# Output-norm sums two blocks later and spread over a block, three output gates held back, decay rows in float32r, memory scaling on GpSimd, in a decoder-layer kernel

## The chip, the core and the metric

The kernel runs on one core of a Trainium2 chip. A core has five engines that run side by side and wait for each other through semaphores: TensorE (PE in the profile; PEld is its weight load), VectorE (DVE), ScalarE (ACT), GpSimd (POOL) and SyncE (SP), which here only issues transfers. The metric is the device time of one execution in microseconds. Before the change it is 1560.88 us, the median of three runs between 1558.69 and 1561.04.

## The reference

The kernel computes one layer of a hybrid decoder for 256 prompt tokens and 8 sampled tokens (264 columns), with a model width of 2048, all in float32:

```python
xn = rmsnorm(x, g_mix);  z = xn @ w_in          # rgx 1024, rgg 1024, q 512, k 512, v 1024, o 1024, gates 8
h_rg = rglru(causal_conv(z_rgx), ...)           # RG-LRU group
y_rg = rmsnorm(h_rg * gelu(z_rgg), g_rg_out)
q, k, v, logi, logf = ...                       # mLSTM group: 4 heads, key 128, value 256
logD = bcum[:, None] - bcum[None, :] + li ;  m_t = max(...)   # running maximum of the gates
qk = (q @ k.T) * exp(logD - m_t)                # prompt: chunkwise; sample: state C0 (8 x 4 x 128 x 256)
h_ml = rmsnorm(num / max(|den|, exp(-m_t)), g_ml_out)         # per head, over 256 values
y_ml = h_ml * sigmoid(z_o)
x = x + concat(y_rg, y_ml) @ w_out
mk, mv = rmsnorm(mem) @ w_k, rmsnorm(mem) @ w_v # 256 memory tokens
x = x + cross_attention(rmsnorm(x) @ w_q, mk, mv) @ w_o       # sample tokens use cached memory keys
x = x + swiglu(rmsnorm(x));  y = rmsnorm(x)
```

The output also has the new states of both groups and the memory keys and values.

## The kernel before

**Tiling.** Activations lie with the features on the 128 partitions and the 264 tokens along the row. Each weight matrix is streamed in column blocks of 128 columns, 1 MB each for 2048 rows. The matrices of the first projection come as rgx (blocks 0 to 7), gates (block 8, half as long), q and k (9 to 16), v (17 to 24), rgg (25 to 32) and o (33 to 40); then `w_out`, the memory projections, cross attention and the feed-forward part follow.

**Weights.** SP loads each block as two halves (`raw`, five buffers). A half is split into two float32r parts by `split_half`: ACT copies it into the high part of a tile `W` (ACTIVATE `W<-raw`), and DVE subtracts to get the low part (TENSOR_TENSOR `W<-raw,W`). There are four `W` tiles, so ACT may write the next one only when PE has read the oldest. `mm3` multiplies one 128-row chunk by three matmuls (high by high, high by low, low by high) into a PSUM bank. A full block has 16 chunks, so 48 of these weight matmuls; in what follows a place on PE is given as the count of weight matmuls before it. Block 9 begins at 416, and each block from there on to block 40 takes 48.

**Banks.** Four PSUM banks, `mm`, take the blocks in turn, and four, `ax`, take all side work. Block i writes the bank that block i-4 used, so its first matmul waits until the result of block i-4 has been read out.

**Order.** The loop over `steps` writes block after block. At the start of a block it evacuates the block before (`pend`, with high priority), then splits the halves of a later block, writes the matmuls, and lets side generators run (`pump`): `rg_gen` (RG-LRU), `ml_gates` (decays of the mLSTM), `ml_prompt` (four heads of the prompt), the sample head states, `ml_norm` (norm of the mLSTM output), `mem_gen` (memory norm). `later` and `drip` put a few small matmuls between two chunks of a block. A list scheduler then sets each engine's order; each engine runs its instructions in that order.

**Places that the change touches.** `first_norm` sums the squares of x over partitions (`token_sums`, six matmuls of one column with `ones`), and spreads the root over the tile (`spread`). `ml_prompt` spreads each head's decay row with one float32 matmul (`bc`), whose stationary operand is a broadcast column of `ident`. A head of `ml_prompt` takes an `ax` bank for the decay (`bc`), one for the scores (`sps`) and one for the numerator (`nps`). The sample states (`ml_sample`) write a small table of decays and vectors to a scratch in memory (`scr`), read it back broadcast (`B<-scr`), fetch the states (`B<-c0T`) and write them back (`o_sc<-B`), all on POOL's queue. `ml_norm` sums each head's squares (`ax<-ones,B`) at the start of block 31. `mem_gen` multiplies 16 chunks of the memory by the reciprocal root (`B<-B,lt`) on DVE and splits each (`B<-B,vecs`).

Of the kernel before, what the change touches and what calls it, by code (L numbers as in the profile page):

```python
# [17 lines left out]
P = 128  # L18
# [65 lines left out]
def layer_kernel(ctx: ExitStack, tc, xT, memT, vec, wrg, w_in, w_out, w_q, w_k, w_v, w_o,  # L84
# [131 lines left out]
    def mm3(ps, a, b, start, stop):  # L216
        ah, al = a
        bh, bl = b
        pe.matmul(ps, ah, bh, start=start, stop=False)
        pe.matmul(ps, ah, bl, start=False, stop=False)  # L220
        pe.matmul(ps, al, bh, start=False, stop=stop)

    st = {}

# [69 lines left out]
    dve.memset(ones, 1.0)  # L294
    ones_r = const.tile([P, P], F32R, name="ones_r")
    dve.tensor_copy(ones_r, ones)
    warm_act = const.tile([P, 1], F32, name="warm_act")
    act.activation(warm_act, ones[:, 0:1], AF.Square)

# [10 lines left out]
    vecs = const.tile([P, NV], F32, name="vecs")  # L310
    act.dma_start(vecs[:, 0:16], vec[:, 0:16])
    act.dma_start(raw_half(0, 0)[:, 0:512], w_in[0][:, 0:512])
    act.dma_start(vecs[:, 16:], vec[:, 16:])

    def V(name, j=0, w=1):
        o = _V[name][0] + j
# [273 lines left out]
    def ml_gates():  # L590
# [14 lines left out]
        dve.tensor_tensor_scan(M[:, :T], g[:, :T], g[:, :T], 0.0, op0=OP.max, op1=OP.max)  # L605
        dve.tensor_add(b[:, :T], b[:, :T], M[:, :T])
        dve.tensor_scalar(M[:, :T], M[:, :T], -1.0, None, op0=OP.mult)
        dve.tensor_copy(mrow[:, 0:1], b[:, T - 1: T])

        s = slice(T, N)  # L610
# [52 lines left out]
    def ml_prompt():  # L663
        qk = ml["qk"]
        yield STEP
        kt = B([P, 2, H, P])
        for tb in range(2):
            ps = bank("ax")
            for h in range(H):
                pe.transpose(ps[:, h * P: h * P + P], qk(4 + h)[:, tb * P: tb * P + P], ident)  # L670
            act.activation(kt[:, tb].rearrange("p h d -> p (h d)"), ps, AF.Copy)
            yield STEP
        while "gates" not in ml or not ml["gates"].done:
            yield STEP
        R = ml["R"]
        M = R(6)[0:4, :T]
        for h in range(H):
            sel = ident[0:4, h: h + 1].to_broadcast([4, P])
            bc = bank("ax")
            pe.matmul(bc[:, :T], sel, M, start=True, stop=True)  # L680
            sps = bank("ax")
            q, k = qk(h), qk(4 + h)
            pe.matmul(sps[:, 0:256], k[:, 0:P], q[:, 0:T], start=True, stop=True)
            pe.matmul(sps[:, 256:384], k[:, P:T], q[:, P:T], start=True, stop=True)
            w = B([P, 1024])
            E, Pm, kw = w[:, 0:384], w[:, 384:768], w[:, 768:1024]
            ml["w", h] = (Pm, kw)
            yield STEP
            dve.tensor_scalar(E[:, 0:256], bc[:, 0:T], gcol[:, 0, h: h + 1], 0.0, op0=OP.add, op1=OP.min)
            dve.tensor_scalar(E[:, 256:384], bc[:, P:T], gcol[:, 1, h: h + 1], 0.0, op0=OP.add, op1=OP.min)  # L690
            act.activation(E, E, AF.Exp)
            dve.tensor_mul(E[:, 0:128], E[:, 0:128], mask)
            dve.tensor_mul(E[:, 256:384], E[:, 256:384], mask)
            dve.tensor_mul(Pm, sps[:, 0:384], E)
            act.activation(kw[:, 0:P], kt[:, 0, h, :], AF.Copy, scale=E[:, 255:256])
            act.activation(kw[:, P:T], kt[:, 1, h, :], AF.Copy, scale=E[:, 383:384])
            yield 1.0
            ml["pn"] = h + 1
# [118 lines left out]

    def ml_norm():

        while not (ml["pg"].done and ml["sg"].done):  # L820
            yield STEP
        hh = hT["t"]
        a = B([P, H, N])
# [21 lines left out]
                dve.tensor_mul(f, f, r)  # L845
            return i

        k = later(*[lambda h=h: sums(h) for h in range(H)])
        while k[1]:
            yield STEP  # L850
        for h in range(H):
# [19 lines left out]
    def proj(src, rhs, evac, cols=2048, n=N, need=()):  # L871

        def f(i):
            ps = bank()
            w = W(i)
            nch = cols // P
            for c in range(nch):
                d = st.pop("drip", None)
                if c == 0:
                    d = st.get("edge")  # L880
                if d is None:
                    mm3(ps[:, :n], w(c), rhs(c), c == 0, c == nch - 1)
                else:
                    with tc.issue_after(d.ins):
                        mm3(ps[:, :n], w(c), rhs(c), c == 0, c == nch - 1)
                drip()
            return ps
        steps.append((src, cols, f, evac, need))

# [86 lines left out]
    def mem_gen():  # L976
# [12 lines left out]
        st["mem"] = Side()  # L989
        for c in range(KC):  # L990
            x = raw(c)
            dve.tensor_mul(x, x, r)
            split(*st["mem"](c), x, V("g_mem", c))
            yield 0.7

# [306 lines left out]
            sp.dma_start(r[:, h % 2 * 512: h % 2 * 512 + 512], w_in[0][:, h * 512: h * 512 + 512])  # L1302
    for q in range(1, 4):
        load_x(4 * q, 4 * q + 4)
        if q < 3:
            load_piece(q)

# [26 lines left out]
    def first_norm():  # L1334
# [11 lines left out]
            act.activation(rstd, ps[:, :N], AF.Copy)  # L1346
            return i

        later(sums, after=4)
        k = later(scale, after=9)  # L1350
        while k[1]:
            yield STEP
        yield 0.1
# [2 lines left out]
    for i, (src, cols, pef, evf, need) in enumerate(steps):  # L1356
        load_piece(i + LD - 1)
        if i == 5:
            finish(lambda: fn.done)
            st["rg"] = side(rg_gen(), 0)  # L1360
        for q in need:
            if q in st:
                finish(lambda: st[q].done)
        if i != 4:
            with tc.high_priority(300):
                for e, x in pend:
                    e(x)
# [10 lines left out]
                    square(q)  # L1378
        if i == 3:
            fn = side(first_norm(), -1)  # L1380
        if i == 5:
            with tc.issue_after(st["split"].ins), tc.issue_after(st["low"].ins):
                rg_coef()
        if evf is not None:
# [120 lines left out]
```

## Time and profile before

| what | value |
|---|---|
| runs | 1558.69, 1560.88, 1561.04 us; median 1560.88 us |
| profiled execution | 1558.76 us |
| its span | 1557.1 us (1.66 us lie outside it) |
| granted clock | 0.995 |
| PE busy | 1537.7 us (99%) |
| DVE busy | 1055.1 us (68%) |
| ACT busy | 781.7 us (50%) |
| POOL busy | 123.1 us (8%) |
| chain that ended last | PE 96%, DVE 2%, ACT 1%, DMA 1% |

The span is the time between the first and the last recorded instruction. A timeline row gives the start of a group of like instructions, the time from the start of the first to the end of the last, the engine, the line, the operation, the tile names (written before the arrow, read after it), the shape, the count, and in brackets how long the engine had been idle and whose work ended the wait. All operations recorded by the helper have line L63.

### The profile page before, as it was taken

Reading aid. Unit: us, or ns where it says so; the run is one execution under the profiler, and the core shown is the slowest. Engines: PE = TensorE matmul, PEld = TensorE weight load, DVE = VectorE, ACT = ScalarE, POOL = GpSimd, SP = SyncE. Lnnn points to the kernel's source line nnn. Section 1 sums busy time; section 2 is a strip of 40 time slices with the busy share of each in tenths; the row PEclk is TensorE's granted clock in tenths of the full one; section 3 lists DMA queues with packets and bytes.
Section 4 is the critical chain, followed back from the end, with each engine's and each line's share of the span. In section 5 each row is a group of like instructions: output and inputs, shape, how many; then the busy total and the mean of one; then the engine's idle time right before and its main releaser. Section 6 shows DMA issues by size and latency. Waiting matters only on the chain.

```text
span 1557.1 us, 30109 instructions
## 1 busy us (share of the span) xinstructions
PE 1537.7 (99%) x12094; PEld 1502.1 (96%) x12094; DVE 1055.1 (68%) x1998; ACT 781.7 (50%) x1229; POOL 123.1 (8%) x190
## 2 busy tenths in 40 slices
PE   9999989999999999999999999999999999999997
PEld 8999989999999888899999999999999999999997
DVE  7976977787699989876665555455555555555554
ACT  6565755665455566655544444334444433444463
POOL 0001210000133343310000000000000000000000
PEclk9999989999999999999999999999999999999999
DMA  7647974547789887955555555555555555555463
GB/s 292 195 154 245 304 259 147 185 157 242 254 303 342 324 299 250 336 166 177 184 178 181 189 178 189 180 186 183 183 186 180 185 182 187 180 188 179 160 183 104
DMA packets 92171, 326.00 MB, mean 209 GB/s; under 512 B 10784, under 2 KB 11216, under 8 KB 92032
## 3 DMA queue, kind: packets, MB, share of 16 engines
q1 hardware_dynamic: 76464, 270.44, 51.5%
q0 software_dynamic: 15136, 53.16, 9.4%
q8 instruction: 94, 1.54, 0.4%
q10 hardware_dynamic: 432, 0.50, 0.1%
q14 instruction: 45, 0.37, 0.1%
HBM read 312.78 MB, written 11.28 MB: 208 GB/s over the span
## 4 chain that ended last, share of the span: by engine, by line
PE 96%; DVE 2%; ACT 1%; DMA 1%; issue 0%; DVEq 0%; ACTq 0%
PE mm L63 91%; PE ax L63 5%; DVE B L63 1%; DVE W L63 1%; ACT W L63 0%; DMA xres<-xT 0%; DMA vecs<-vec 0%; ACT B L63 0%; ACT t L63 0%; DVE c L63 0%; DVE xres L63 0%; DVE acc_x L63 0%; DVE t L63 0%; ACT rstd L63 0%; DVEq L1482 0%
## 5 line engine op out<-in xcount | busy, mean ns | idle before, releaser
L63 PE MATMUL mm<-B,W 128*128 128x264 f32 (+2 forms) x11008 | 1368.0, 286 | 1.7 <-DVE W L63 0.8
L63 PEld LDWEIGHTS mm<-B,W 128*128 128x128 f32 x11008 | 1343.7, 188 | 13.9 <-DVE W L63 1.0
L63 DVE TENSOR_TENSOR W<-raw,W 128x1024 fp32r<-128x1024 f32 (+2 forms) x518 | 622.3, 1204 | 363.5 <-ACT W L63 362.9
L63 ACT ACTIVATE W<-raw 128x1024 fp32r<-128x1024 f32 (+2 forms) x518 | 536.6, 1038 | 661.1 <-PE mm L63 461.6
L63 PE MATMUL mm<-W,B 128*128 128x512 f32 x384 | 92.7, 395 | 0.0
L63 PEld LDWEIGHTS mm<-W,B 128*128 128x128 f32 x384 | 70.9, 188 | 15.9
L63 DVE TENSOR_TENSOR t<-mm,rstd 128x264 f32<-128x264 f32 x104 | 44.9, 433 | 45.0 <-PE mm L63 44.5
L1397 POOL TENSOR_TENSOR B<-B,rstd 128x264 f32<-128x264 f32 x4 | 2.8, 744 | 855.1 <-ACT rstd L63 855.1
L63 DVE TENSOR_TENSOR xres<-xres,mm 128x264 f32<-128x264 f32 x80 | 34.3, 429 | 38.6 <-PE mm L63 38.6
L63 DVE SCALAR_TENSOR_TENSOR B<-B,dw 128x256 f32<-128x256 f32 x128 | 55.6, 490 | 4.0 <-ACT dw L63 4.0
L63 DVE SCALAR_TENSOR_TENSOR dw<-B,qsm,dw 128x256 f32<-128x256 f32 x96 | 49.8, 527 | 0.4
L63 PE MATMUL ax<-B,B 128*128 128x256 f32 (+3 forms) x288 | 48.2, 308 | 0.1
L63 PEld LDWEIGHTS ax<-B,B 128*128 128x128 f32 x288 | 40.6, 190 | 3.4 <-issue 0.6
L1046 POOL TENSOR_TENSOR dr<-dw,dr 128x256 fp32r<-128x256 f32 x32 | 34.1, 1070 | 106.9 <-ACT dr L63 105.8
L63 ACT ACTIVATE B<-xres,vecs 128x264 fp32r<-128x264 f32 (+1 forms) x64 | 31.1, 503 | 3.6 <-DMA vecs<-vec 1.5
L1035 POOL DMA_DIRECT2D B<-kcT x32 | 17.3, 541 | 146.3 <-DVE B L63 137.4
L63 ACT ACTIVATE B<-t 128x264 fp32r<-128x264 f32 (+1 forms) x60 | 24.3, 410 | 4.3 <-DVE t L63 4.2
L63 ACT ACTIVATE t<-xres 128x264 f32<-128x264 f32 x45 | 18.6, 414 | 15.4 <-DVE xres L63 15.4
L63 ACT ACTIVATE dw<-B,qsm 128x256 f32<-128x256 f32 x32 | 16.2, 507 | 17.8 <-DVE B L63 10.9
L63 ACT ACTIVATE t<-t 128x264 f32<-128x264 f32 (+1 forms) x61 | 24.9, 408 | 0.6 <-DVE t L63 0.5
L63 DVE SCALAR_TENSOR_TENSOR B<-xres,vecs,B 128x264 fp32r<-128x264 f32 x48 | 22.6, 491 | 3.7 <-ACT B L63 3.7
L63 ACT ACTIVATE t<-B,B 128x128 f32<-128x128 f32 x64 | 21.4, 389 | 4.8 <-DMA B<-scr 4.8
(153 smaller groups left out, 657.0 us busy)
## 6 DMA issues: line engine op xcount, KB each, us to landing
raw<-w_gu SPq DMA_DIRECT2D x176, 512.0 KB, 3.5
raw<-w_in SPq DMA_DIRECT2D x80, 512.0 KB, 4.3
raw<-w_d SPq DMA_DIRECT2D x80, 512.0 KB, 3.6
raw<-w_out SPq DMA_DIRECT2D x32, 512.0 KB, 3.7
B<-kcT POOLq DMA_DIRECT2D x32, 512.0 KB, 8.4
raw<-w_q SPq DMA_DIRECT2D x32, 512.0 KB, 4.2
B<-vcT POOLq DMA_DIRECT2D x32, 512.0 KB, 8.4
raw<-w_k SPq DMA_DIRECT2D x32, 512.0 KB, 6.9
```

Of the source, the lines that this page charges most:

```text
L63: return f(*a, **k)
L1035: pool_e.dma_start(kc, kcT[h, b])
L1046: pool_e.tensor_sub(wr[:, 1], acc, wr[:, 0].bitcast(F32))
L1397: e.tensor_mul(st["y"](c), st["y"](c), r)
```

## The change

There are six edits.

1. First norm: `vecs[:, 16:]` is loaded from SP's queue behind the second quarter of x; it was on ACT's queue. The token sums go in after eight drips (four before) and the spread ten drips later (nine). `finish(fn.done)` and the start of `rg_gen` are one block apart from where they were: `rg_gen` begins at block 5 and the norm's end is required at block 6, and blocks 4 and 5 both skip the evacuation.
2. A drip is issued after the matmul of its chunk (`issue_after(m.ins)`).
3. `ml_norm` starts only from block 33 on (`st["i"] < 33`), and its four sums begin after three drips.
4. Blocks 34 and 35 skip the evacuation, so the first three output gates (blocks 33 to 35) are evacuated at the start of block 36.
5. The decay rows: the row M is split into two float32r parts (`mhl`, one ACT copy and one DVE subtraction of 4x256), `ident_r` is a float32r copy of four rows of `ident`, and a decay is spread by two float32r matmuls in place of the float32 one.
6. The 16 multiplications of `mem_gen` are put on POOL (`pool_e.tensor_mul`).

```diff
@@ mm3 @@
-        pe.matmul(ps, al, bh, start=False, stop=stop)
+        return pe.matmul(ps, al, bh, start=False, stop=stop)
@@ constants @@
+    ident_r = const.tile([4, H], F32R, name="ident_r")
+    dve.tensor_copy(ident_r, ident[0:4, 0:H])
...
-    act.dma_start(vecs[:, 16:], vec[:, 16:])
@@ ml_gates @@
+        mhl = ml["mhl"] = B([P, 2, T], F32R)[0:4]
+        act.activation(mhl[:, 0], M[:, :T], AF.Copy)
+        dve.tensor_sub(mhl[:, 1], M[:, :T], mhl[:, 0].bitcast(F32))
@@ ml_prompt @@
-            sel = ident[0:4, h: h + 1].to_broadcast([4, P])
+            sel = ident_r[:, h: h + 1].to_broadcast([4, P])
             bc = bank("ax")
-            pe.matmul(bc[:, :T], sel, M, start=True, stop=True)
+            pe.matmul(bc[:, :T], sel, mhl[:, 0], start=True, stop=False)
+            pe.matmul(bc[:, :T], sel, mhl[:, 1], start=False, stop=True)
@@ ml_norm @@
-        while not (ml["pg"].done and ml["sg"].done):
+        while not (ml["pg"].done and ml["sg"].done) or st["i"] < 33:
             yield STEP
...
-        k = later(*[lambda h=h: sums(h) for h in range(H)])
+        k = later(*[lambda h=h: sums(h) for h in range(H)], after=3)
@@ proj @@
                 if d is None:
-                    mm3(ps[:, :n], w(c), rhs(c), c == 0, c == nch - 1)
+                    m = mm3(ps[:, :n], w(c), rhs(c), c == 0, c == nch - 1)
                 else:
                     with tc.issue_after(d.ins):
-                        mm3(ps[:, :n], w(c), rhs(c), c == 0, c == nch - 1)
-                drip()
+                        m = mm3(ps[:, :n], w(c), rhs(c), c == 0, c == nch - 1)
+                if drips:
+                    with tc.issue_after(m.ins):
+                        drip()
@@ mem_gen @@
-            dve.tensor_mul(x, x, r)
+            pool_e.tensor_mul(x, x, r)
@@ loads at the start @@
+        if q == 2:
+            sp.dma_start(vecs[:, 16:], vec[:, 16:])
@@ first_norm @@
-        later(sums, after=4)
-        k = later(scale, after=9)
+        later(sums, after=8)
+        k = later(scale, after=10)
@@ loop over the blocks @@
         if i == 5:
+            st["rg"] = side(rg_gen(), 0)
+        if i == 6:
             finish(lambda: fn.done)
-            st["rg"] = side(rg_gen(), 0)
...
-        if i != 4:
+        st["i"] = i
+        if i not in (4, 5, 34, 35):
             with tc.high_priority(300):
                 for e, x in pend:
                     e(x)
...
-        if i == 5:
+        if i == 6:
             with tc.issue_after(st["split"].ins), tc.issue_after(st["low"].ins):
                 rg_coef()
```

Three places show how the order moves.

PE at the sums of the output norm. Before, they stand behind the first chunk of block 31 (`mm_2873`, from weight matmul 1472):

```order
L63 MATMUL mm_2873<-B_137,W_2797 128x264
L63 MATMUL mm_2873<-B_138,W_2797 128x264
L63 MATMUL mm_2873<-B_137,W_2797 128x264
L63 MATMUL ax_2856<-ones,B_2699 128x1 x3
L63 MATMUL mm_2873<-B_137,W_2797 128x264
L63 MATMUL mm_2873<-B_138,W_2797 128x264
L63 MATMUL mm_2873<-B_137,W_2797 128x264
L63 MATMUL ax_2856<-ones,B_2699 128x1 x3
```

In the change they stand in block 35 (`mm_3153`, from weight matmul 1664), behind the second part of the RG-LRU group's sums (`ax<-ones,acc_rg`):

```order
L63 MATMUL mm_3153<-B_139,W_3063 128x264 x2
L63 MATMUL mm_3153<-B_140,W_3063 128x264
L63 MATMUL mm_3153<-B_139,W_3063 128x264
L63 MATMUL ax_3123<-ones,acc_rg 128x1 x3
L63 MATMUL ax_3143<-ones,B_3038 128x1 x3
L63 MATMUL mm_3153<-B_163,W_3063 128x264
L63 MATMUL mm_3153<-B_164,W_3063 128x264
L63 MATMUL mm_3153<-B_163,W_3063 128x264
L63 MATMUL ax_3143<-ones,B_3038 128x1 x3
```

The four groups of sums moved by some 200 weight matmuls, from 1475 to 1676.

DVE at the evacuation of one rgg block (`t<-mm,rstd`) among the sample states (`B<-B,bcs,t` and the sums into `nums`). Before, it is the result of block 27 (`mm_2536`), behind the low half `W_2867`, whose tile PE gives up at weight matmul 1448; block 31 needs the bank at 1472:

```order
L63 TENSOR_TENSOR W_2867<-raw_2786,W_2867 128x8x128
L63 SCALAR_TENSOR_TENSOR B_2504<-B_2504,bcs,t_2618 128x256
L63 SCALAR_TENSOR_TENSOR t_2622,nums<-B_2504,B_2505 128x128
L63 TENSOR_TENSOR t_2625<-mm_2536,rstd 128x264
L63 SCALAR_TENSOR_TENSOR t_2622,nums<-B_2504,B_2505 128x128
L63 TENSOR_TENSOR W_2870<-raw_2788,W_2870 128x8x128
```

In the change the same group of rows takes the result of block 28 (`mm_2604`), behind `W_2916`, whose tile PE gives up at weight matmul 1520; block 32 needs the bank at 1520:

```order
L63 TENSOR_TENSOR W_2916<-raw_2830,W_2916 128x8x128
L63 SCALAR_TENSOR_TENSOR B_2545<-B_2545,bcs,t_2671 128x256
L63 SCALAR_TENSOR_TENSOR t_2675,nums<-B_2545,B_2546 128x128
L63 TENSOR_TENSOR t_2678<-mm_2604,rstd 128x264
L63 SCALAR_TENSOR_TENSOR t_2675,nums<-B_2545,B_2546 128x128
L63 TENSOR_TENSOR B_1696<-B_1696,t_2678 128x264
```

What moved is the tile ahead of the evacuation: one block of sample states more lies behind it, and the distance between the tile's release and the need of the bank went from 24 weight matmuls to none.

PE at weight matmul 1136, where the third head's decay is spread (`ax<-B,ident`, now `ax<-B,ident_r`) and its scores computed. Before, the block's own matmuls (`mm_2162`) follow at once, and the numerators of the first head (`ax_2105`) stand at 1158:

```order
L63 MATMUL ax_2093<-B_945,ident 128x256
L63 MATMUL ax_2095<-B_946,B_1262 128x256
L63 MATMUL ax_2095<-B_946,B_1262 128x128
L63 MATMUL mm_2162<-B_137,W_2026 128x264
L63 MATMUL ax_2099<-ident,B_1916 128x128 x4
L63 MATMUL mm_2162<-B_138,W_2026 128x264
```

In the change the first head's numerators (`ax_2066`, four rows from there on) stand ahead of the block's matmuls (`mm_2116`):

```order
L63 MATMUL ax_2053<-B_1171,ident_r 128x256 x2
L63 MATMUL ax_2056<-B_934,B_1254 128x256
L63 MATMUL ax_2056<-B_934,B_1254 128x128
L63 MATMUL ax_2060<-ident,B_1876 128x128 x4
L63 MATMUL ax_2066<-B_1859,B_1537 128x256
L63 MATMUL ax_2066<-B_1859,B_1537 128x128
L63 MATMUL ax_2066<-B_1859,B_1537 128x256
L63 MATMUL ax_2066<-B_1859,B_1537 128x128
L63 MATMUL mm_2116<-B_139,W_1986 128x264
```

The bank of `ax_2066` is given up by DVE's product of the second head's scores with the decay. The transposes of the gates and of the table for `scr` also moved, each by one block: from 848 to 896 and from 944 to 992, while the decay spreads kept their places (1040, 1088, 1136 and 1184).

On POOL the 16 multiplications of the memory stand behind the loads of the memory (`B<-memT`) and ahead of the first `B<-kcT`; the second write-back `o_sc` of a state now stands ahead of the third load `B<-c0T`, where four loads stood ahead of the first write-back before.

More of the change, by code (lines that the diff above doesn't have):

```diff
@@ L674, in ml_prompt @@
             yield STEP
-        R = ml["R"]
-        M = R(6)[0:4, :T]
+        mhl = ml["mhl"]
         for h in range(H):
-            sel = ident[0:4, h: h + 1].to_broadcast([4, P])
+            sel = ident_r[:, h: h + 1].to_broadcast([4, P])
             bc = bank("ax")
-            pe.matmul(bc[:, :T], sel, M, start=True, stop=True)
+            pe.matmul(bc[:, :T], sel, mhl[:, 0], start=True, stop=False)
+            pe.matmul(bc[:, :T], sel, mhl[:, 1], start=False, stop=True)
             sps = bank("ax")
```

## The prediction

> **What bounds the kernel now.** I read the busy shares and the chain of waits first, then the list of TensorE's waits, then the timeline around each wait.
>
> ```profile
> PE 1537.7 (99%) x12094; PEld 1502.1 (96%) x12094; DVE 1055.1 (68%) x1998; ACT 781.7 (50%) x1229; POOL 123.1 (8%) x190
> PE 96%; DVE 2%; ACT 1%; DMA 1%; issue 0%; DVEq 0%; ACTq 0%
> PE ax L63 <- DVE B L63: 4.1, 1, 4.1
> PE ax L63 <- DVE acc_x L63: 1.0, 1, 1.0
> PE mm L63 <- DVE W L63: 0.8, 1, 0.8
> PE mm L63 <- DVE t L63: 0.7, 1, 0.7
> PE ax L63 <- DVE c L63: 0.3, 1, 0.3
> ```
>
> PE is the bound. An edit can gain only where PE stands idle or where PE has less to do, and it can lose by a new wait of PE. The five waits listed here are single events, 6.9 us together, and the edits aim at all five. Their places in PE's timeline, with the bracket at a row's end giving the idle time ahead of it:
>
> ```profile
> 12.90 0.75 PE L63 MATMUL ax<-B,W 128*128 128x264 f32 x4 [0.26 <-ACT W L63]
> 13.85 0.39 PE L63 MATMUL mm<-B,W 128*128 128x264 f32 x1 [0.20 <-ACT W L63]
> 33.84 0.83 PE L63 MATMUL ax<-ones,acc_x 128*128 128x1 f32 x6 [0.96 <-DVE acc_x L63]
> 34.53 3.85 PE L63 MATMUL mm<-B,W 128*128 128x264 f32 x30
> 38.64 0.81 PE L63 MATMUL ax<-ident,c 128*128 128x128 f32 x6 [0.26 <-DVE c L63]
> 212.75 4.95 PE L63 MATMUL mm<-B,W 128*128 128x264 f32 x40
> 218.40 0.60 PE L63 MATMUL mm<-B,W 128*128 128x264 f32 x3 [0.70 <-DVE t L63]
> 223.12 1.41 PE L63 MATMUL ax<-ones,B 128*128 128x1 f32 x6 [4.11 <-DVE B L63]
> 351.53 0.63 PE L63 MATMUL mm<-B,W 128*128 128x264 f32 x3 [0.81 <-DVE W L63]
> ```
>
> Forty weight matmuls in 4.95 us make 0.12 us for one; with this I turn distances on PE into time.
>
> **First norm (edits 1, 2).** It takes away 0.96 + 0.26 = 1.22 us. The sums now stand four drips, 12 matmuls or 1.4 us, further on, which is more than the 0.96 that PE waited. The root's chain on DVE takes 38.64 − 34.53 = 4.11 us from the end of the sums. It now has 33 matmuls, 4.0 us, and in DVE's new order one low half of the weights (1.23 us in a row below) stands ahead of it, partly beside the sums. So a wait of 0.1 to 1.3 us stays; I take 0.3, nearest to the 0.26 of before: **−0.9** (0 to −1.1). The `vecs` load on SP takes a transfer off ACT's start; the waits of PE for ACT's halves at 12.90 and 13.85 (0.26 and 0.20) may hold some of that: **−0.3** (0 to −0.5).
>
> **Decay rows (edit 5).** The four spreads look alike:
>
> ```profile
> 146.63 0.69 PE L63 MATMUL ax<-B,ident 4*128 4x256 f32 x2
> 147.25 0.81 PE L63 MATMUL ax<-B,B 128*128 128x256 f32 x3
> L63 PE MATMUL ax<-dr,ones_r 128*128 128x256 f32 x64 | 17.3, 287 | 0.0
> ```
>
> From start to start a spread takes 0.62 us. Two float32r matmuls of 256 columns take 0.24 by the weight matmuls (nearly the same shape), 0.54 by 17.3/64 = 0.27 from the group of `dr`. Four times the difference is −1.5 or −0.3. I take **−1.4**, since the weight matmuls stand pipelined like these. The copy and the subtraction of 4x256 lie on ACT and DVE in the gates' chain; their cover is the move of the transposes by one block, 5.76 us.
>
> **Output-norm sums (edits 3, 4).** The 4.11 us are DVE's squares and halves ahead of the sums. Two hundred weight matmuls later, 24 us, the sums find the same squares some 1 us earlier than they come on PE, by the rows of DVE's order ahead of them at the prices below. The four sums cost PE the same wherever they stand. The output gates that are held back cost 3 × 0.43 us on DVE at the start of block 36, and the bank of block 33 is needed first at block 37, 5.8 us on, so nothing. The spreads of the norm move to 1749, and `w_out` needs them after block 40. So **−4.1**, and the 0.70 just ahead goes too: **−0.7**. What is late next is the question here: with the sums gone from block 31, DVE's sample states spread out by a block, and the evacuation of block 28 lands behind a low half. This is the group of rows of before that gave the 0.70:
>
> ```profile
> 214.86 1.06 ACT L63 ACTIVATE W<-raw 128x1024 fp32r<-128x1024 f32 x1 [1.23 <-PE mm L63]
> 215.95 1.23 DVE L63 TENSOR_TENSOR W<-raw,W 128x1024 fp32r<-128x1024 f32 x1 [0.59 <-ACT W L63]
> 217.10 0.48 DVE L63 SCALAR_TENSOR_TENSOR B<-B,bcs,t 128x256 f32<-128x256 f32 x1
> 217.61 0.29 DVE L63 SCALAR_TENSOR_TENSOR t<-B,B 128x128 f32<-128x128 f32 x1
> 217.83 0.43 DVE L63 TENSOR_TENSOR t<-mm,rstd 128x264 f32<-128x264 f32 x1
> ```
>
> PE gives up a `W` tile (ACT's wait ends at 214.86), ACT writes the high half, DVE the low half, a state step, a sum, and then the evacuation that frees the bank; PE goes on at 218.40. From ACT's row that is 3.54 us; from the tile's last matmul it is the 24 matmuls that followed (3.0 us at 4.95/40) and the 0.70, so 3.7. Those 24 were the cover, and only 0.7 showed. In the change the same five instructions stand in the same order, but the tile's last reader is the matmul just ahead of the one that needs the bank: nothing covers the chain. **+3.7** (+3.0 if the second state step and the sum were already done, +4.1 with one more). Behind the waiting evacuation on DVE are sums of the RG-LRU norm and the next low half, which is needed 48 matmuls later and stays hidden.
>
> **The head stage (consequence of edits 1 and 5).** The table for the sample states goes to memory one block later, but the heads of the prompt stay:
>
> ```profile
> 135.77 0.56 POOL L782 DMA_DIRECT2D scr<-lt  x1 [0.97 <-ACT den L63]
> 141.89 1.11 POOL L790 DMA_DIRECT2D B<-scr  x2 [5.55 <-DMA scr<-lt]
> 146.94 0.69 ACT L63 ACTIVATE t<-B,B 128x128 f32<-128x128 f32 x2 [4.84 <-DMA B<-scr]
> 161.56 0.69 PE L63 MATMUL ax<-B,ident 4*128 4x256 f32 x2
> ```
>
> The first state operation was at 146.94, and moves by 5.76 to 152.7. From there to the product that frees the first head's bank, DVE has two low halves (2.46), four state steps (1.92), seven sums (2.0), one evacuation (0.43) and the decays of two heads (some 2.9, by the prices of the nearest `B<-B` rows), 9.7 us less an overlap of 0.08 at each of 18 rows: 8.3, so done at 161.4 if ACT is never late, and 163 if each second step waits 0.2 for ACT. PE comes there at 161.56 less two saved spreads (0.76) plus one float32r spread, the scores and four transposes (1.2): 162.0. I take **+1.0** (0 to +4). The later places of this stage tie within 0.5; the third load `B<-c0T` goes out behind two write-backs: **+0.3** (0 to +3).
>
> **Memory scaling (edit 6).** DVE's 16 multiplications leave its path, and the 0.81 with them:
>
> ```profile
> 335.60 5.45 DVE L63 TENSOR_TENSOR B<-B,lt 128x256 f32<-128x256 f32 x16
> L1046 POOL TENSOR_TENSOR dr<-dw,dr 128x256 fp32r<-128x256 f32 x32 | 34.1, 1070 | 106.9 <-ACT dr L63 105.8 <-DVE W L63 1.1
> L1397 POOL TENSOR_TENSOR B<-B,rstd 128x264 f32<-128x264 f32 x4 | 2.8, 744 | 855.1 <-ACT rstd L63 855.1
> 445.39 0.75 POOL L1046 TENSOR_TENSOR dr<-dw,dr 128x256 fp32r<-128x256 f32 x1
> 445.36 1.08 DVE L63 SCALAR_TENSOR_TENSOR B<-B,dw 128x256 f32<-128x256 f32 x1
> 446.37 0.42 DVE L63 SCALAR_TENSOR_TENSOR B<-B,dw 128x256 f32<-128x256 f32 x1
> ```
>
> ACT's order puts one half between each four memory chunks. The last chunk is ready at 335.6 + 16p, p being the price of one on POOL; the half behind it is split some 4.0 us later (ACT's copy, a residual row, 1.06, and DVE's 1.23). PE needs it at weight matmul 2480: from 350.72 (351.53 less 0.81, matmul 2410) 70 × 0.12 on, 359.1. So it is late by 16p − 19.5: nothing at 0.744 or at 1.070, from p = 1.22 on a loss. I take p = 1.07: **−0.8** (+4.2 at the top, below).
>
> **Sum.** −0.9 − 0.3 − 1.4 − 4.1 − 0.7 − 0.8 = −8.2; +3.7 + 1.0 + 0.3 = +5.0; together −3.2 us. Against the profiled execution's 1558.76 that is 1555.6; the median of the runs is 2.1 above it, and with the same −3.2 I predict 1557.7.
>
> **The rivals.** *A, the full gain.* The bank of block 28 is free in time, or nearly, as before (0.7), and the head stage ties: −8.2 + 0.7, so 1553.4. For it: before, the same rows cost only 0.70. Against: the cover was the distance of 24 matmuls, and the order now leaves none.
>
> *B, slower: the table for the sample states is late.* The whole 5.76 us of its move show at the first head's bank, since state steps stand ahead of the decay products on DVE, and the third state's load is late by 3: −8.2 + 3.7 + 5.8 + 3.0 = +4.3, 1565.2. For it: POOL waited 5.55 and ACT 4.84 us for these transfers. Against: by the sum above DVE catches up with PE to about a microsecond. It decides from some 7.6 us of wait between weight matmuls 1136 and 1232 on.
>
> *C, DVE and POOL shut each other out.* The last three rows above show a DVE operation of two inputs, 0.42 alone, taking 1.08 as it meets one of POOL's. If each low half (1.23) and four splits (0.42 each) shut out POOL for their whole time, four multiplications take 4 × 0.75 + 2.91 = 5.9 us, p = 1.48, and the last half is late by 4.2 in place of a gain of 0.8: 1557.7 + 5.0 = 1562.7. Against: the mean of 32 such operations, many beside low halves, is 1.07.
>
> [...]
>
> **How the numbers follow.** My forecast has 0.55, A 0.13, B 0.12, C 0.13; 0.07 is left for what I don't see. A measurement of this kernel tells about 0.2% (3.1 us) from no change, so faster is below 1557.8, slower above 1564.0. The forecast lies on the lower edge; by itself it goes from 1555 to 1560.5, with 0.31 faster and 0.24 the same. A is faster. B is slower. C is the same with 0.10 and slower with 0.03; of the rest 0.03 are faster, 0.02 each the same and slower. Faster 0.47, same 0.36, slower 0.17. The range takes in A nearly whole and C: 1552.5 to 1564.
>
> **What would show it.** In the changed kernel's timeline: sums of the output norm with no idle time ahead of them; a wait of 3.7 us of PE for DVE's `t` at the first matmul of block 32, near 218 to 224 us; no wait over 1 us at 34 to 40; four spreads of 0.25; a wait for `B` at the first head's numerators near 162, of 0 to 4 us; POOL's 16 multiplications at about 1.07 and no wait for `W` near 350 to 360. I am wrong if the 3.7 is absent (A), if the waits from 155 to 185 sum to over 5 (B), or if PE waits for `W` while POOL multiplies (C).

## The result, and the profile after

The changed kernel takes 1555.49 us (median of 14 runs, 1552.79 to 1559.36) against 1560.68 us for the kernel before on the same chips (14 runs, 1558.69 to 1562.27). The ratio is 0.997, 95% interval 0.9962 to 0.9979: 5.2 us faster, where 1557.7 and a gain of 3.2 us had been forecast. The profiled execution of the change took 1558.61 us, one of its longer ones, so its trace tells where waits stand, and not what the median is made of. The granted clock is the share of its full rate that TensorE got; the longer of the 14 runs have the lower one: spans of 1551.1 to 1554.6 us came at 0.994 or 0.995, those of 1556.5 to 1557.6 us at 0.992 or 0.993.

TensorE's waits in the change:

```profile
PE mm L63 <- DVE t L63: 3.6, 1, 3.6
PE ax L63 <- DVE B L63: 1.7, 1, 1.7
PE mm L63 <- DVE ones L63: 1.1, 1, 1.1
PE mm L63 <- DVE W L63: 1.1, 1, 1.1
PE mm L63 <- ACT W L63: 0.5, 1, 0.5
```

Their places in PE's timeline, and the first norm and a decay spread beside them:

```profile
13.66 0.75 PE L63 MATMUL mm<-B,W 128*128 128x264 f32 x4 [0.45 <-ACT W L63]
34.00 0.72 PE L63 MATMUL ax<-ones,acc_x 128*128 128x1 f32 x6
38.64 0.73 PE L63 MATMUL ax<-ident,c 128*128 128x128 f32 x6
144.74 0.49 PE L63 MATMUL ax<-B,ident_r 4*128 4x256 f32 x2
145.17 0.92 PE L63 MATMUL ax<-B,B 128*128 128x256 f32 x4
162.74 2.89 PE L63 MATMUL ax<-B,B 128*128 128x256 f32 x8 [1.72 <-DVE B L63]
227.41 20.50 PE L63 MATMUL mm<-B,W 128*128 128x264 f32 x156 [3.58 <-DVE t L63]
249.44 0.72 PE L63 MATMUL ax<-ones,B 128*128 128x1 f32 x6
350.58 40.65 PE L63 MATMUL mm<-B,W 128*128 128x264 f32 x334 [1.06 <-DVE W L63]
```

The forecast's shape is all here: the sums of the output norm no longer wait (249.44), the first norm's 0.96 and 0.26 are gone, PE waits 3.58 for DVE's `t` at block 32, 1.72 for the first head's bank near 162, and once for a weight half at 350. The five waits that the edits aimed at sum to 6.8 us in the timeline of before; those for `t`, `B` and `W` that stand in their place sum to 6.4. By idle time alone hardly anything is gained, and this pair of profiles shows no gain at all: the spans are 1557.1 us before and 1556.9 after, one of the shorter executions of before against one of the longer of the change. What differs besides the waits is the clock. Stretches of PE before and after; behind the time come the busy times of PE, PEld, DVE, ACT and POOL, and the third number from the right is the granted clock. Before:

```profile
222.00:226.00 4.00, 2.88 (x14) 2.91 (x14) 3.67 (x13) 2.56 (x9) 2.62 (x5) 0.57 0.75 243
226.00:230.00 4.00, 4.00 (x21) 4.00 (x20) 1.75 (x5) 1.19 (x3) 0.00 (x0) 0.50 0.99 332
230.00:234.00 4.00, 4.00 (x23) 4.00 (x24) 2.40 (x14) 0.87 (x1) 0.00 (x0) 0.65 0.36 147
```

In the change:

```profile
164.00:168.00 4.00, 4.00 (x24) 3.79 (x24) 3.96 (x13) 3.10 (x8) 0.00 (x0) 0.72 0.68 246
228.00:232.00 4.00, 4.00 (x23) 4.00 (x23) 3.19 (x14) 2.18 (x7) 0.00 (x0) 0.61 0.65 212
250.00:254.00 4.00, 4.00 (x26) 4.00 (x26) 3.24 (x22) 0.35 (x1) 0.00 (x0) 0.70 0.61 215
254.00:258.00 4.00, 4.00 (x20) 4.00 (x19) 1.65 (x4) 0.70 (x1) 0.00 (x0) 0.50 0.25 90
258.00:262.00 4.00, 4.00 (x34) 4.00 (x33) 3.14 (x10) 1.65 (x3) 0.00 (x0) 0.95 0.10 41
```

PE reads as fully busy in nearly all of these rows, but at 0.50 it does little more than half the matmuls (20 in the four microseconds from 254 us, where before has 36 at 1.00). Adding up one minus the clock over slices of half a microsecond, the wait of 4.11 before was followed by 4.9 us of lost time; the change loses 1.7 behind the wait of 1.72, 1.7 behind the wait of 3.58, 3.4 at its sums (250 to 260 us), and 1.2 from 1545.21 us to the end of its last matmul at 1547.67 (before, the clock falls at 1550.38, behind the last matmul, and costs nothing there). My sum had no term for any of it. In this pair of executions the change thus loses more to the clock than the kernel before, 8.0 against 4.9 us; where the 5.2 us between the medians come from is told by the experiments, not by this pair.

### The profile page after: what moved, and what is told of

Same layout as the page of the kernel before. It is cut to its first block, busy times and chain, and to the rows that moved or that the text cites. A ratio compares the mean times of both kernels' runs of the same rounds, so it can differ in the third digit from the quotient of the medians.

```text
span 1556.9 us, 30113 instructions
## 1 busy us (share of the span) xinstructions
PE 1539.4 (99%) x12094; PEld 1505.2 (97%) x12094; DVE 1057.4 (68%) x1984; ACT 782.5 (50%) x1230; POOL 140.4 (9%) x206
## 4 chain that ended last, share of the span: by engine, by line
PE 96%; DVE 2%; DMA 1%; ACT 1%; issue 0%; DVEq 0%; SPq 0%; ACTq 0%; POOLq 0%
PE mm L63 91%; PE ax L63 5%; DVE B L63 1%; DVE W L63 1%; DMA raw<-w_in 1%; DMA B<-scr 0%; DMA scr<-lt 0%; ACT W L63 0%; DMA vecs<-vec 0%; ACT B L63 0%; ACT t L63 0%; ACT L63 0%; DVE t L63 0%; DVE xres L63 0%; DVE acc_x L63 0%
## 5 line engine op out<-in xcount | busy, mean ns | idle before, releaser
L998 POOL TENSOR_TENSOR B<-B,lt 128x256 f32<-128x256 f32 x16 | 15.6, 1012 | 94.5 <-ACT lt L63 94.5
```

What stands on the lines that cost most here:

```text
L998: pool_e.tensor_mul(x, x, r)
```

## The experiments

Each was timed against the kernel before on the same chip; "before" is that median, 1560.6 to 1560.8 us. Each has four or five runs (edit 5 alone eleven), so two experiments that differ by less than some 2 us are not told apart by their times.

### The evacuation on another ring of tiles

```diff
 def evac_rgg(n):
-            z = tmp()
+            z = ltmp()
             dve.tensor_mul(z, ps[:, :N], rstd)
```

> The change, with one edit: the rgg evacuation takes its tile from the other ring of temporaries (lt), which the sample states do not use. Theory 1 (the order put the evacuation of block 28 behind the low half W_2916 because both use the ring t, and a long wait also halves PE's clock for some microseconds): the wait of 3.58 us at block 32 is gone, and with it the 1.7 us lost to the clock at 226 to 232 us, so about 5.3 us less than the change and some 10 us less than before. Rival (the bank is late for another reason, or the clock's loss comes at random places): the wait stays or turns up at the next block, or only 3.6 us are gained because the clock drops elsewhere.

Measured 1549.73 us, ratio 0.993 (0.9917 to 0.9942): 10.9 us under before and 5.8 under the change. No wait is left at block 32 (the 384 matmuls from 192.77 us run through it without idle time), and the clock is full up to 244 us:

```profile
34.35 0.83 PE L63 MATMUL ax<-ones,acc_x 128*128 128x1 f32 x6 [0.76 <-DVE acc_x L63]
162.03 1.58 PE L63 MATMUL ax<-B,B 128*128 128x256 f32 x8 [0.54 <-DVE B L63]
192.77 46.25 PE L63 MATMUL mm<-B,W 128*128 128x264 f32 x384
245.08 6.21 PE L63 MATMUL mm<-B,W 128*128 128x264 f32 x27
```

A ring is a set of buffers that are handed out in turn. The evacuation's tile shared the ring `t` with the sample states, so it could not stand ahead of them; from the other ring the scheduler puts it in time. The price of the wait was its length and the clock behind it (3.58 and 1.7 us in the change's profile). What stays is the stretch behind the sums: 27 weight matmuls take 6.21 us at 245 us, 3.3 at full clock.

### The sums four chunks apart

```diff
-        k = later(*[lambda h=h: sums(h) for h in range(H)], after=3)
+        for h in range(H):
+            k = later(lambda h=h: sums(h), after=3)
```

(on top of the experiment before)

> As gate_ring, and the four sums of the output norm stand four chunks apart (12 weight matmuls) in place of one. Theory 1b (24 one-column matmuls in a row with few weight matmuls between them look like an idle PE, so the clock is halved at 250 to 260 us, 3.4 us lost): that stretch shows the full clock, 3.4 us less than gate_ring. Rival (that stretch is the phase of whatever sets the clock): the loss is there or not without regard to the distance, and the median is that of gate_ring within 1 us.

Measured 1547.26 us, ratio 0.9915 (0.9901 to 0.9928), 2.5 us under the one before. The stretch in the two kernels, `gate_ring`:

```profile
244.00:248.00 4.00, 4.00 (x22) 4.00 (x21) 2.00 (x8) 1.06 (x1) 0.00 (x0) 0.53 0.46 189
248.00:252.00 4.00, 4.00 (x24) 4.00 (x23) 1.33 (x6) 0.63 (x1) 0.00 (x0) 0.62 0.41 131
```

and with the sums apart:

```profile
242.00:246.00 4.00, 4.00 (x36) 4.00 (x35) 2.03 (x6) 1.06 (x1) 0.00 (x0) 1.00 0.94 384
246.00:250.00 4.00, 4.00 (x36) 4.00 (x35) 2.36 (x7) 1.65 (x3) 0.00 (x0) 1.00 0.41 138
```

The same 24 one-column matmuls, with the same number of weight matmuls around them, cost the clock where only three of those stand between two groups (0.53 and 0.62 above), and do not with twelve (1.00). PE never stood idle there. The other profiles agree: three with three between (`gate_ring`, the change and the memory scaling back on DVE) have a low stretch of 3.4 or 6.8 us there, four with twelve have none. The medians, 2.5 us apart, say it less surely. With all 24 in one go the outcome was mixed: a low stretch of 3.4 us at 247.5 us in the next experiment, none at 243 us with edits 3 and 4 alone. Why this is so was not tried.

### The first norm as before

Edits 1 and 2 taken back:

```diff
-        later(sums, after=8)
-        k = later(scale, after=10)
+        later(sums, after=4)
+        k = later(scale, after=9)
...
-        if i not in (4, 5, 34, 35):
+        if i not in (4, 34, 35):
```

> The change without edits 1 and 2 (first norm, its loads and drips as before), all else kept. Theory 1c (the first norm's edit moves the sample states one block later and so makes both new waits): the 1.72 at the head stage and the 3.58 at block 32 are gone with their clock losses (8.7 us together), the waits of the first norm come back (0.96 + 0.26), and the 0.70 at block 31: some 5 to 6 us less than the change. Rival (the waits come from the moved sums, edit 3): both stay, and the time is 1 to 2 us above the change.

Measured 1553.44 us, ratio 0.9953 (0.994 to 0.9965), 2.0 us under the change (the runs of the two overlap), not the 5 to 6 expected. Half of the theory stands: the wait of 3.58 is gone, with two of 0.71 in its place. The other half fell: the head stage waits as long as in the change, though the table for the sample states goes out one block earlier.

```profile
33.85 0.83 PE L63 MATMUL ax<-ones,acc_x 128*128 128x1 f32 x6 [0.96 <-DVE acc_x L63]
164.97 0.66 PE L63 MATMUL ax<-ident,B 128*128 128x128 f32 x4 [1.68 <-DVE B L63]
219.50 5.99 PE L63 MATMUL mm<-B,W 128*128 128x264 f32 x48 [0.71 <-DVE t L63]
226.20 17.50 PE L63 MATMUL mm<-B,W 128*128 128x264 f32 x144 [0.71 <-DVE t L63]
```

### The memory scaling back on DVE

```diff
-            pool_e.tensor_mul(x, x, r)
+            dve.tensor_mul(x, x, r)
```

(in the change)

> The change with the 16 memory multiplications back on DVE (edit 6 undone). Theory: GpSimd and DVE shut each other out there, so DVE's low halves go back from 1.76 to 1.23 us, PE's wait near 350 us from 1.06 to 0.8, and the time is that of the change within 0.5 us. Rival (edit 6 is a gain of 0.8 as forecast): 0.8 us slower than the change.

Measured 1555.48 us, ratio 0.9966 (0.9952 to 0.9979): the change's median to 0.01 us. Edit 6 is worth nothing that five runs can tell; by the time alone a gain of 0.8 is not excluded. The traces show no gain at its place: PE's wait near 350 us is 0.82 with DVE and 1.06 with GpSimd, and over all profiles with sixteen splits it is 0.80 to 0.82 in five with DVE (before among them) and 1.05 to 1.06 in four with GpSimd. The rows of the change beside it, with one of before ahead of them:

```profile
342.10 1.28 DVE L63 SCALAR_TENSOR_TENSOR B<-B,vecs,B 128x256 fp32r<-128x256 f32 x3
```

```profile
336.58 1.76 DVE L63 TENSOR_TENSOR W<-raw,W 128x1024 fp32r<-128x1024 f32 x1
338.26 2.72 DVE L63 SCALAR_TENSOR_TENSOR B<-B,vecs,B 128x256 fp32r<-128x256 f32 x3
341.79 1.76 DVE L63 TENSOR_TENSOR W<-raw,W 128x1024 fp32r<-128x1024 f32 x1
333.81 15.63 POOL L998 TENSOR_TENSOR B<-B,lt 128x256 f32<-128x256 f32 x16 [94.52 <-ACT lt L63]
```

A low half takes 1.76 us in place of 1.23, three splits 2.72 in place of 1.28. GpSimd multiplies from 333.81 to 349.44 us, and behind that two splits take 0.87 again. Added up, DVE's rows beside GpSimd are some 7.6 us longer (1.6 on three low halves, 4.0 on nine splits, 2.0 on four other rows), against the 5.45 us that DVE was spared. In this experiment's profile, with all 16 on DVE, a low half among the splits took 1.22 us and three splits 1.27.

### Edits 1 and 2 alone

The first norm's part of the diff on the kernel before, nothing else.

> Before with edits 1 and 2 alone (first norm, its loads and drips). Theory 2 (these edits move the sample states one block later, and that alone puts the evacuation of block 28 behind W_2916): the 0.96 and 0.26 at 34 to 39 us go, a wait of about 3.6 for t appears at block 32 though the sums of the output norm were not moved on purpose, it takes the place of the 0.70, a wait of 1 to 2 appears at the head stage, and the sums right behind keep the clock's loss near 5 us: 1 us faster to 1 us slower than before. Rival (the wait at block 32 belongs to the move of the sums, edit 3): no such wait here, the 4.11 stays, and the time is 1.2 us under before.

Measured 1565.17 us, ratio 1.0032 (1.0019 to 1.0044): 4.4 us slower than before.

```profile
163.75 1.57 PE L63 MATMUL ax<-B,B 128*128 128x256 f32 x8 [1.39 <-DVE B L63]
218.53 6.00 PE L63 MATMUL mm<-B,W 128*128 128x264 f32 x48 [0.71 <-DVE t L63]
228.10 1.00 PE L63 MATMUL mm<-B,W 128*128 128x264 f32 x3 [3.57 <-DVE t L63]
235.85 1.41 PE L63 MATMUL ax<-ones,B 128*128 128x1 f32 x6 [6.76 <-DVE B L63]
```

The wait of 3.57 at block 32 comes with the first norm, not with the move of the sums: the rival is out. And it stands beside the 0.71 and lengthens the wait of the sums (6.76 in place of 4.11); by the order of the rows the sample states, whose results they need, have moved back a block. It is worse than the theory's "1 us either way": I had the 3.6 replace the 0.70, and had not followed the sums. In the change the move of the sums hides the second of these.

### Edits 3 and 4 alone

```diff
-        while not (ml["pg"].done and ml["sg"].done):
+        while not (ml["pg"].done and ml["sg"].done) or st["i"] < 33:
...
-        if i != 4:
+        st["i"] = i
+        if i not in (4, 34, 35):
```

(and `after=3` at the four sums)

> Before with edits 3 and 4 alone (output-norm sums from block 33 on, three gates held back). Theory: the 4.11 goes, the 0.70 stays, no wait above 1 us is added, and the clock's loss of 5.1 us at 222 to 234 us shrinks to what the sums alone cost (0 to 3.4, all ten groups of sums stand together at one place here): 5.8 to 9 us under before. Rival (a wait costs its own length and no clock): 4.1 under before.

Measured 1551.84 us, ratio 0.9949 (0.9935 to 0.9962): 8.95 us under before, twice the 4.11. No stretch of low clock is left between 165 and 1540 us.

```profile
164.95 0.66 PE L63 MATMUL ax<-ident,B 128*128 128x128 f32 x4 [1.66 <-DVE B L63]
220.13 23.25 PE L63 MATMUL mm<-B,W 128*128 128x264 f32 x192 [0.70 <-DVE t L63]
243.36 2.82 PE L63 MATMUL ax<-ones,B 128*128 128x1 f32 x24
```

So this edit is worth more than the whole change. Edits 3 and 4 were not parted. The run also shows where the head stage's wait is from. Up to there the order of each engine's rows is that of before, where no wait showed; here it is 1.66. What differs is a transfer: ScalarE's first row on the table of the sample states is at 146.94 before (4.84 us of waiting, the row shown with the prediction), and here

```profile
149.94 0.70 ACT L63 ACTIVATE t<-B,B 128x128 f32<-128x128 f32 x2 [7.79 <-DMA B<-scr]
```

Three microseconds later, of which 0.39 lie in the issue of the read (142.28 in place of 141.89 us). In the seven profiles with the order of the change here, PE is released 10.9 or 11.0 us after this row of ScalarE in six, and 11.35 in one; the row itself comes at 150.3 to 151.9 us. So the wait at the head stage goes by the landing of the read from `scr`, which varies from one execution to the next, less the time at which PE arrives.

### Edit 5 alone

The five lines of the diff on `mhl` and `ident_r`, on the kernel before.

> Before with edit 5 alone (decay rows in float32r). Theory from the trace of the change (a spread takes 0.43 us from start to start in place of 0.62): 0.76 us under before if no wait is added, so within 1 us of before; and PE comes sooner to the head stage, where a wait for DVE's B of up to 1 us may eat it. Rival (my forecast's 0.24 a spread): 1.4 under before.

Measured 1561.74 us, ratio 1.0007 (0.9998 to 1.0016): no change that can be told. A spread takes 0.43 us in place of 0.62, as in the change. In its profile PE comes sooner to its next waits (1.31 near 164, and 5.40 for the sums where 4.11 stood), and these take it back, with some more at the clock (low for 13.7 us in place of 10.2).

### The memory in two bursts

```diff
-            pool_e.tensor_mul(x, x, r)
+            dve.tensor_mul(x, x, r)
             split(*st["mem"](c), x, V("g_mem", c))
-            yield 0.7
+            yield STEP if c % 2 else 0.7
```

(on top of the sums apart)

> sums_apart with the memory multiplications on DVE and the splits of the memory in two bursts of eight chunks in place of sixteen. Theory (PE's wait for W near 340 us comes from sixteen splits that stand ahead of two weight halves): the wait of 1.06 goes or falls under 0.3, so 1 us under sums_apart. Rival (the wait is due to the multiplications themselves): 0.8 stays.

Measured 1546.13 us, ratio 0.9907 (0.9893 to 0.9921): 1.1 us under the sums apart, less than these runs can tell; but the wait for `W` is gone, here and in both kernels of the next experiment, which have this order. It is the best version run: 14.7 us under before and 9.4 under the change, with no wait of PE above 0.4 us behind the first two microseconds.

### Eight waits of two lengths

What a wait costs was still argued from single events. Two kernels put eight waits of one length into blocks 130 to 200 of the best version:

```diff
+        if i in range(130, 210, 10):
+            z, zb = tmp(), bank("ax")
+            with tc.high_priority(300):
+                dve.tensor_copy(z, ps[:, :N])
+                for _ in range(2):
+                    dve.tensor_max(z, z, z)
+                st["edge"] = pe.matmul(zb[:, 0:1], z[:, 0:P], ones[:, 0:1], start=True, stop=True)
         ps = pef(i)
```

(`range(7)` in the second)

> sums_apart_mem_in_two with eight waits of PE put into the projections of cross attention and the feed-forward part (blocks 130 to 200, each tenth): ahead of the block a one-column matmul waits for a copy of the block before and two more operations on DVE (0.43 us each, 1.5 to 2.5 us of wait with the semaphores and a low half that may stand ahead). What is added is not part of the layer. Theory 3 (PE's clock is set by windows of some 3.4 us; a wait halves it for one window, 1.7 us lost, only if most of a window falls into the wait): each wait costs its length, and few of the eight (0 to 3) cost 1.7 more: 14 to 22 us in all. Rival (every wait above 1 us costs a window): 8 x (2 + 1.7) = 30 us.

> The same eight places with seven operations in place of two, five times 0.43 us more: waits of 3.7 to 4.7 us. Theory 3: nearly every wait now costs one or two windows of 1.7 us: 8 x 2.2 = 17 us more for the waits, and 8 to 24 us more for the clock than with the short ones. Rival (a wait costs its length alone, and the clock losses seen so far came from the one-column sums): 17 us more and no stretch of low clock in the profile.

Measured 1589.36 us (ratio 1.0179, 1.0162 to 1.0196) and 1607.73 us (1.0297, 1.0279 to 1.0314): 43.2 and 61.6 us over the best version. Two waits of the short kernel, and two of the long:

```profile
1014.57 0.35 PE L63 MATMUL ax<-ones,t 128*128 128x1 f32 x2 [2.90 <-DVE t L63]
1075.36 0.56 PE L63 MATMUL ax<-ones,t 128*128 128x1 f32 x2 [2.84 <-DVE t L63]
```

```profile
1023.78 0.56 PE L63 MATMUL ax<-ones,t 128*128 128x1 f32 x2 [5.24 <-DVE t L63]
1088.70 0.56 PE L63 MATMUL ax<-ones,t 128*128 128x1 f32 x2 [5.18 <-DVE t L63]
```

and the clock behind the two short ones:

```profile
1016.00:1020.00 4.00, 4.00 (x36) 4.00 (x35) 0.94 (x1) 1.06 (x1) 0.00 (x0) 1.00 0.22 74
1078.00:1082.00 4.00, 4.00 (x21) 4.00 (x21) 0.00 (x0) 0.51 (x1) 0.00 (x0) 0.53 0.00 0
```

The low stretches, read in slices of half a microsecond, come in two lengths, 3.4 and 6.8 us at half clock. Of the eight short waits (2.80 to 2.90 us) one had no low stretch, four had 3.4 us, three 6.8; all eight long ones (5.13 to 5.24 us) had 6.8. Lost once the wait was over: 16.5 us behind the short ones (0 to 3.3 each) and 16.3 behind the long ones (1.9 to 2.5 each, since a part of the low stretch lies within the wait). With the waits, 22.9 and 41.6, that is 39.4 and 57.9. Of the rest of some 4 us, 1.7 are the added matmuls (0.21 for a pair at full clock), and 1.1 and 0.8 were lost ahead of the first of them (the group that starts at 782.22 us in the best version starts at 783.36 and 782.99 here); about 1 is not traced to a place. Both rivals fall: not each wait brings a low stretch (2.90 at 1014.57 brought none), and a wait does not cost its length alone (16.5 and 16.3 us were lost on top). My own theory's sizes fell too: I said that few of the short waits (0 to 3) would cost 1.7 us more, and behind seven the clock fell; and the long ones lose no more clock than the short ones, only more time.

## Why the prediction was right, and where its steps were not

The time (1555.49 in 1552.5 to 1564, forecast 1557.7) and the sign were right. Most terms stood in the right place. That the sum came out only 2 us off is in part luck, since its omissions had both signs: the clock behind the wait removed (4.9 us of gain) and the clock behind the new waits and at the sums (1.7, 1.7 and 3.4 in the profiled execution; less in most, to go by their granted clock).

The medians of three kernels part the change by edits. Edits 3 and 4 alone give −8.9 us; with 5 and 6 added, the kernel with the first norm as before, +1.6; with 1 and 2 added, which is the change, +2.0. The last two steps are no larger than what these runs can tell apart, so the gain is that of edits 3 and 4, and the times show none from the other four. The forecast had edits 1 and 2 at −1.2, 5 at −1.4 and 6 at −0.8.

- **Output-norm sums, −4.1 and −0.7.** Right in place, short in size: the wait was followed by a half clock that cost 4.9 us, which the timeline of before showed and I did not read. Alone, the edit gave 8.95 us. This is the term of the sum that was mis-sized most. The sums moved from block 31 to block 35, four blocks; the two of the title are how much later `ml_norm` may begin. That they cost PE the same wherever they stand, as the step says, does not hold either: they cost 3.4 us of clock at the new place. The 0.70 is gone in the change, but stays with edits 1 and 2 alone and with edits 3 and 4 alone.
- **Block 32, +3.7.** Measured 3.58, by the chain named: in the rows below ACT goes on at 223.87 us, as PE's wait begins, and PE at 227.41, which is 3.54 us as in the rows of before. What the step lacked is again the clock (1.7 in the profiled execution; the experiment that removed the wait gained 5.8 us between the medians). It also laid the wait to the sums' move; edits 1 and 2 alone show it at 3.57, so it belongs to the first norm's edit.
- **First norm, −0.9.** In the change's profile both waits are gone (−1.2); of seven other kernels with these edits, three still waited 0.63 to 0.76 for the sums. As an edit it costs 4.4 us by itself, by what it does two hundred microseconds later. I costed it at its own place and put its distant cost under another edit.
- **The start, −0.3.** The two waits of 0.26 and 0.20 became one of 0.45, and one of 0.64 at 6.13 us of before, which the step does not list, is gone. But over all profiles PE's waits for ACT's halves here sum to 0 to 1.1 us without the edit and 0 to 0.6 with it, so no gain can be told. (In the code the `vecs` load stands behind the third quarter of x, not the second.)
- **Decay rows, −1.4.** 0.43 in place of 0.62, four times: −0.76. That is 0.21 a matmul, between the 0.12 of the weight matmuls that I went by and the 0.27 of the group of `dr`; the lower bound of the step was nearer. In the time of edit 5 alone not even the 0.76 shows.
- **Head stage, +1.0 (0 to +4).** 1.72 in the change, 0.38 to 0.93 in six other profiles of its order. The product on DVE was done at 162.7, within the 161.4 to 163 of the step, but its parts were off: the first state operation came at 151.87, not 152.7, and PE at 161.02, not 162.0, and the chain between took 10.9 us, where the step's terms add up to 8.3 (from 152.7 that makes 161.0, not the 161.4 that it says). But the cause as I put it, the table's move by one block, is not needed: the kernel with the table in the old place waits 1.66 as well, at the transposes a little further on, when the read from `scr` lands late. The late third load, +0.3, left no wait.
- **Memory scaling, −0.8.** No gain: the times are equal with the multiplications on either engine. GpSimd took 0.98 us each (15.63 us for 16), below the 1.22 from which I expected a loss; what the step left out is the other side, DVE's low halves at 1.76 (1.22 with the multiplications on DVE). That is rival C's collision at a small price: PE's wait is 0.25 us longer in place of 0.8 shorter.

The chain at block 32 in the change:

```profile
223.87 1.06 ACT L63 ACTIVATE W<-raw 128x1024 fp32r<-128x1024 f32 x1 [1.23 <-PE mm L63]
224.96 1.23 DVE L63 TENSOR_TENSOR W<-raw,W 128x1024 fp32r<-128x1024 f32 x1 [0.57 <-ACT W L63]
226.10 0.48 DVE L63 SCALAR_TENSOR_TENSOR B<-B,bcs,t 128x256 f32<-128x256 f32 x1
226.62 0.29 DVE L63 SCALAR_TENSOR_TENSOR t<-B,B 128x128 f32<-128x128 f32 x1
226.83 0.43 DVE L63 TENSOR_TENSOR t<-mm,rstd 128x264 f32<-128x264 f32 x1
```

Of the rivals, A (no new wait, 1553.4) did not come, though its time is as near to the median (2.1 us) as the forecast's (2.2): the time alone would not have told the two apart, the wait does. B (1565.2) did not come, as DVE caught up; C came in part. Of the things that would show the steps, the 3.7 us wait, the sums without idle time and the head's wait were seen; "four spreads of 0.25" and "no wait for `W` near 350" were not.

The row that would have caught the main error stands in the timeline of before:

```profile
226.33 1.01 PE L63 MATMUL mm<-B,W 128*128 128x264 f32 x3
```

Three weight matmuls, 1.01 us; three like them take 0.60 at 218.40. PE counts as busy in both.

## What to carry to other kernels

A wait of the bounding engine is not priced by its idle time (taking away 4.11 us of wait gave 8.95 here): look at the granted clock of the ten microseconds behind it, and at the duration of a like group of matmuls before and after. An edit at one place of a scheduled program should be costed at every place whose rows it moves, and a read-out that stands late may do so only because its tile shares a ring with other work; giving it another ring was worth 5.8 us here for one word. Moving work from a busy engine to an idle one gained nothing here (1555.49 against 1555.48 us), where the busy engine's own instructions took longer beside it (1.76 us for a low half in place of 1.22).

## What the runs showed of the hardware

TensorE's granted clock fell to half (0.50) for 3.4 us or for 6.8 us, never for another length in the eighteen stretches read closely behind waits of 1.7 to 5.2 us that no sums followed; with sums behind a wait it was longer (10.2 us before, 13.7 with edit 5 alone, 20.5 with edits 1 and 2 alone), always a multiple of 3.41. Waits of up to 1.1 us left it at 1.00 in all twelve profiles (the last 12 us of a trace aside); waits of 1.3 to 1.7 left it four times of five; waits of 2.8 to 2.9 brought it down seven times of eight, and those of 5.1 to 5.2 always. The same order gave different losses from one execution to the next: the wait at block 32 was followed by 1.7 us lost in the change, and by 2.7 with the memory scaling back on DVE.

The clock's record in the traces shows what goes with that. Within one trace the low stretches begin whole multiples of 3.41 us apart, whatever the waits do: at 162.82, 227.67 and 251.56 us in the change, which are 19 and 7 times 3.41, and at 825.75, 890.61 and 952.05 us with the eight short waits, 19 and 18 times. Each of the seven short waits that lowered the clock had 2.4 to 2.8 us in the 3.41 us just ahead of the low stretch. The eighth, of 2.90 us up to 1014.57, lies across such a boundary, at 1013.49 (midway between the low stretches at 952.05 and 1074.93, which are 36 times 3.41 apart), with 1.8 us on one side and 1.1 on the other. And in all eighteen the low stretch lasted 6.8 us where the wait ran on by 0.29 us or more past the boundary, and 3.4 where by 0.17 or not at all. So the price of a wait here went by its length and by where it fell on this grid.

Of these 3.41 us just ahead of a low stretch, 2.1 to 2.8 us of wait were enough, 1.72 us were once (at the head stage of the change; waits of 1.66 and 1.68 there, in two other kernels, brought no low stretch), and 24 one-column matmuls with three weight matmuls between two groups brought the clock down without any idle time. What sets the lengths, the spacing and the two levels was not shown.

The clock would also explain, by my estimate, the spread of the change's runs (6.6 us between the lowest and the highest, 3.6 before): they differ in the granted clock, 0.992 to 0.995. It was not tried. At the end of the ten traces without the eight waits the clock is low once more (0.50). In all but the change this begins behind the last matmul (at 1550.38 us before, 1541.28 with the evacuation's tile on the other ring) and costs nothing; in the change's profile it begins 2.5 us ahead of it, and the last twelve matmuls take 2.62 us in place of 1.87. What sets that was not tried either.
